# Three more Strassen steps in B's and the FFNs' output products, one column half of the FFNs with its steps in another order, and a new buffer from a smaller dynamic DMA scratch

## The chip, the cores and the metric

The kernel runs on one core of one Trainium2 chip. The metric is the device time of one execution in microseconds, as the median of several runs. Before the change it is 2434.19 us, a median of 3 runs from 2432.38 to 2434.53 us.

## The reference

The program is one layer of a streaming encoder on 256 tokens of width 2048, in float32: a half-weighted SwiGLU feed-forward block (FFN), a mixer with two attention branches A and B, cross attention to 256 memory tokens, and a second FFN, each followed by a layer norm over the scaled residual.

```python
h = layer_norm(ALPHA * h + 0.5 * swiglu_ffn(h, ffn1_w_in, ffn1_w_out), ...)
mix = (g_a * (A(h) @ w_o_a) + g_b * (B(h) @ w_o_b)) @ w_out
h = layer_norm(ALPHA * h + mix, ...)
xa = memory_cross_attention(h, mem, ...)        # ... @ w_xo
h = layer_norm(ALPHA * h + xa, ...)
h = layer_norm(ALPHA * h + 0.5 * swiglu_ffn(h, ffn2_w_in, ffn2_w_out), ...)

def swiglu_ffn(x, w_in, w_out):
    g, u = jnp.split(x @ w_in, 2, axis=-1)      # 5504 columns each
    return (jax.nn.silu(g) * u) @ w_out
```

The three products that matter here are `ffn1_w_out`, `w_o_b` (2048 x 2048) and `ffn2_w_out` (5504 x 2048).

## The kernel before

Every large product runs in split precision. A float32 operand is cut into a high part (a cast to `fp32r`, done by ACT at L262 for weights, L253 for activations) and a low part (what is left, a subtraction by DVE at L265 or L254), and a product is three matmuls: high by high, low activation by high weight, high activation by low weight. The two parts of a weight lie in the tiles `hi` and `lo`, of which there are two each (`UNITS`); a raw weight of 1 MB lies in one of three `raw` tiles, loaded from HBM by SP's queue (L191). A new load starts when the DVE has read the last of the weight that lay in the tile. SP's queue also carries the DMA transposes (L845).

The work goes in **steps**. One step is two blocks of 128 rows of a weight, by 1024 columns, for all 256 tokens. `pair_group` (L643) lays out the steps of one group of 1024 columns, which has 4 output tiles in PSUM (two halves of tokens by two of columns). A plain step is `mm_pair` (L301): 8 block products of three matmuls, so 24 matmuls of 512 columns (L309). A Strassen step is `mm_sums` (L345): its 2 x 2 blocks need 7 block products, 21 matmuls (L363). It takes sums of weight blocks, which the DVE forms (`weight_sums`, L244, at L246 and L248) and splits like a weight into two tiles (for instance X2 and X3), and sums of activation blocks, here called **forms** (`sum_forms`, L314, at L319 and L323, split at L253 and L254), which are kept in a buffer called the form's home. Four of its products go to four shared PSUM tiles `qs`; after a group's last Strassen step `shared` (L669) reads these (L674 to L679) and combines them. The tables `SUMS_OUT`, `AT_YB` and so on say which steps of a group are Strassen steps. Two kinds of PSUM tile, `mm` and `at`, of four each, take turns as a group's own and as its shared tiles.

The instructions of an engine stand in a fixed order when the program is built. The order is made by a scheduler from the order of the calls and from priorities. So an instruction that must wait holds up all that stands behind it on its engine, and a changed step can move its neighbours.

Three places are touched:

- **FFN output, first 24 row blocks** (`ffn`, L551): 12 steps in each of two column halves. Steps 3, 5, 7 and 9 are Strassen steps in both. Behind a half, `finish` (L743) adds the four output tiles to the residual `h` (L749).
- **B's output** (`out_b`, L1268): two column halves of 8 steps, `w_o_b`. Steps 2, 4 and 6 are Strassen steps in the first half, 4 and 6 in the second. Its `done` (L1271) adds the shared tiles (L1276), multiplies by the gate (L1277), adds A's half (L1278), and ACT then splits the words into planes (L841). They are transposed by a DMA, joined again by ACT (L849) and split (L253, L254) into the blocks X0, X1, T0 and X3 of the next product's operand.
- **`w_out`** (`out`, L1316) follows directly: 8 steps for each column half. Its steps 0 to 3 read X0 and X1, made from the first half of B's output; its steps 4 and 5 read T0, and 6 and 7 X3, made from the second. Into its steps are woven the statistics of the memory's layer norm (`mem_norm`, BN_STATS at L387), whose inputs `mem` and `memT` POOL's queue loads (L1334, L1336).

Of the kernel before, what the change touches and what calls it, by code (L numbers as in the profile page):

```python
# [28 lines left out]
AT_FIRST = 4, 6  # L29
SUMS_OUT = ({3: ("X1", 0), 5: ("X1", 1), 7: ("X0", 0), 9: ("X0", 1)},  # L30
            {3: ("X1", 0), 5: ("X1", 1), 7: ("X0", 0)})
SUMS_YB = {4: ("T0", 0), 6: ("T0", 1), 2: None}
AT_YB = (2, 4, 6), (4, 6)
SUMS_XQ = {4: ("H5", 0), 6: ("H5", 1), 2: None}
SUMS_XV = {4: ("T3", 0), 6: ("T3", 1), 2: None}
SUMS_XO = {2: None, 4: ("H2", 0), 6: ("H2", 1)}
# [3 lines left out]
SUM_HOME = ("X2", "X3"),  # L40
# [59 lines left out]
class Kernel:  # L100
# [450 lines left out]
    def ffn(self, tag, xT, st, first=None, steps=None, late=None, before=None, tags=None):  # L551
# [5 lines left out]
        fx = {}  # L557
        for half, nf in enumerate(F_SPLIT):
# [33 lines left out]
            def out(hid=hid):  # L592
                x = lambda: hid
                src = [t[tag + "_w_out"][g, :, f0 * 1024:(f0 + nf) * 1024] for g in range(2)]
                self.out_pair(bank, src[0], 0, nf, x, homes, fh, half == 0, st if end else None,
                              SUM_HOME + ("H5",) if end else SUM_HOME)
                if end:
                    self.out_proj(tag + "_w_out_r", nf, x, False, st, steps, tags, 2, cut=tags is None)
                else:
                    self.out_pair(bank ^ 1, src[1], 1, nf, x, homes, fh, half == 0, None)  # L600
            main = self.collect(out)

            side = dict(turn)
# [2 lines left out]
            for c, (home, k) in homes.items():  # L606
                if home == "X0":
                    side[4 + 2 * k] = side.get(4 + 2 * k, []) + [form(c)]
            if not end:
                for i in range(2):  # L610
                    side[len(main) - 3 + i] = [self.forms_step(fx, SUMS_IN, tuple(SUMS_IN)[i], xT)]
            self.weave(main, side, prio=0)
            turn = None
            f0 += nf

    def out_pair(self, bank, src, g, nk, x, at, fx, scale, st, sums_in=SUM_HOME):

        nc, h = self.nc, self.h
        ps, qs = {}, {}

        def shared():
            for (tt, a), s in qs["add"].items():
                c = (2 * g + a) * 512
                hs = h[tt][:, c:c + 512]
                if scale:
                    nc.vector.scalar_tensor_tensor(hs, hs, ALPHA, s, ALU.mult, ALU.add)
                else:
                    nc.vector.tensor_tensor(hs, hs, s, ALU.add)

        def finish():  # L630
            for tt in range(2):
                for a in range(2):
                    self.finish(tt, 2 * g + a, ps[tt, a], scale and not at, st)
        self.pair_group(bank, src, 512, nk, x, at, fx, ps, qs, shared, sums_in)
        self.add(finish)

    def group_tile(self, j):
# [2 lines left out]
    def group_tiles(self, j):  # L640
        return {(tt, g): self.group_tile(j) for tt in range(2) for g in range(2)}

    def pair_group(self, bank, src, n, nk, x, at, fx, ps, qs, then=None, sums_in=SUM_HOME):  # L643


        steps = -(-nk // 2)
        sums = [c for c in range(steps) if c in at]
        for c in range(steps):
            kts = range(2 * c, min(2 * c + 2, nk))
            ap = src[:, kts[0] * 2 * n:(kts[-1] + 1) * 2 * n]  # L650
            if c in at:
                def fn(w, c=c):
                    if c == sums[0]:
                        qs.update((a, self.group_tile(bank + 1)) for a in range(4))
                    self.mm_sums(ps, qs, w, n, x(), fx[c], 2 * c, c == sums[0], c == sums[-1])
                self.add(fn, Sums(ap, *sums_in))
                if c == sums[-1]:
                    self.add(lambda: self.shared(qs, n), prio=SOON)
                    if then:
                        self.add(then)  # L660
                continue

            def fn(w, c=c, kts=kts):
                if c == 0:
                    ps.update(self.group_tiles(bank))
                self.mm_pair(ps, w, n, x(), kts, c == 0, c == steps - 1)
            self.add(fn, ap)

    def shared(self, qs, n):  # L669
# [1023 lines left out]
def _layout(i):  # L1693
    import numpy as np
    a = {k: np.asarray(v) for k, v in i.items()}
    r = {}
# [5 lines left out]
    for f in ("ffn1", "ffn2"):  # L1702
        w = a[f + "_w_in"][0]
        r[f + "_w_in"] = _pairs(
            w[:, D_FF:D_FF + NG * 512], w[:, :NG * 512], 512, [AT_FIRST] + [SUMS_IN] * (NG - 1))
        r[f + "_w_in_r"] = _pairs(
            w[:, D_FF + NG * 512:], w[:, NG * 512:D_FF], D_FF - NG * 512, [SUMS_IN])
        w = a[f + "_w_out"][0]
        at = [*SUMS_OUT[0], *(F_SPLIT[0] // 2 + c for c in SUMS_OUT[1])]
        r[f + "_w_out"] = _pairs(*_halves(w), 512, [at, at])  # L1710
        r[f + "_w_out_r"] = _tok(w[F_SPLIT[0] * P:, D // 2:])
    r["ffn2_gate"] = _tok(a["ffn2_w_in"][0][:, :512])
    r["ffn2_up"] = _tok(a["ffn2_w_in"][0][:, D_FF:D_FF + 512])
# [57 lines left out]
```

## Time and profile before

| | |
|---|---|
| median of 3 runs | 2434.19 us (2432.38 to 2434.53) |
| the profiled execution: span of its instructions | 2432.9 us; its own time beside the span is not listed |
| PE (matmul) busy | 2423.0 us, 11286 matmuls |
| DVE busy | 2121.1 us |
| ACT busy | 1551.3 us |
| POOL busy | 36.1 us |
| SP's DMA queue (q1) | 495.83 MB |

The span runs from the first to the last instruction of the profiled execution. A row of the timeline has the start in us, the duration, the engine, the source line, the operation with output and input names, the shape and a count of instructions that follow each other; in brackets stands the idle time before it and what ended that. A window row has the busy time of each engine in a stretch. Durations of back-to-back instructions overlap a little: an engine takes up the next one some 0.1 us before the last one's recorded end.

### The profile page before, as it was taken

The page shows a single profiled execution, that of the slowest core. Times are in us where ns is not written, and L with a number is a line of the kernel's source. Part 1 is how long each engine was busy: PE and PEld are TensorE (multiplying, and loading weights), DVE is VectorE, ACT ScalarE, POOL GpSimd, SP SyncE. Part 2 cuts the span into 40 slices and gives each one's busy share as a digit, 9 for nine tenths or more (in the row PEclk, how much of TensorE's full clock was granted, in tenths as well). Part 3 has the DMA queues.
Part 4 walks back from the last instruction along what each step waited for, and adds up shares of the span by engine and source line. Part 5 has one row for each costly group of instructions (what it writes and reads, how often), then busy time and mean ns, then how long its engine had stood idle before and what let it go on. Part 6 is the DMA issues. An engine that isn't in the chain of part 4 may idle for free.

```text
span 2432.9 us, 29701 instructions
## 1 busy us (share of the span) xinstructions
PE 2423.0 (100%) x11286; PEld 2022.5 (83%) x11286; DVE 2121.1 (87%) x2423; ACT 1551.3 (64%) x2017; POOL 36.1 (1%) x81
## 2 busy tenths in 40 slices
PE   9999999999999999999999999999999999999999
PEld 8888888889888888888888888888888888888887
DVE  8999989899878898789788889979879999888997
ACT  6676745666555557878565687765666675556762
POOL 0000000000000001000000000000000000000000
PEclk9999999999999999999999999999999999999999
DMA  7766656666645657776577577655556666666665
GB/s 268 252 214 213 208 199 221 212 199 222 225 172 209 208 209 248 230 209 175 184 249 251 167 236 218 219 184 189 190 199 214 229 221 210 216 208 205 201 223 182
DMA packets 176414, 516.20 MB, mean 212 GB/s; under 512 B 111728, under 2 KB 112496, under 8 KB 121104
## 3 DMA queue, kind: packets, MB, share of 16 engines
q1 hardware_dynamic: 170816, 495.83, 61.2%
q0 software_dynamic: 4592, 17.30, 2.2%
q8 instruction: 88, 1.44, 0.2%
q10 hardware_dynamic: 864, 1.18, 0.1%
q14 instruction: 54, 0.44, 0.1%
HBM read 485.30 MB, written 2.10 MB: 200 GB/s over the span
## 4 chain that ended last, share of the span: by engine, by line
PE 90%; DVE 4%; ACT 3%; DMA 1%; issue 1%; SPq 0%; DVEq 0%; ACTq 0%
PE at L309 24%; PE mm L309 23%; PE mm L296 11%; PE at L363 10%; PE mm L363 10%; PE mm L275 5%; PE mm L277 2%; DVE lo L265 2%; ACT hi L262 1%; PE at L1028 1%; DMA raw<-w_xq 0%; PE at L1499 0%; PE at L1082 0%; PE at L275 0%; DMA raw<-w_o_b 0%
## 5 line engine op out<-in xcount | busy, mean ns | idle before, releaser
L262 ACT CAST hi<-raw 128x1024 fp32r<-128x1024 f32 (+1 forms) x852 | 805.3, 982 | 454.2 <-PE at L309 155.0
L265 DVE TENSOR_TENSOR lo<-raw,hi 128x2048 fp32r<-128x2048 f32 (+1 forms) x427 | 902.3, 2114 | 139.3 <-ACT hi L262 133.4
L309 PE MATMUL mm<-hi,T 128*128 128x512 f32 (+1 forms) x1328 | 311.1, 384 | 1.3 <-DVE v L397 1.3
L309 PEld LDWEIGHTS mm<-hi,T 128*128 128x128 f32 x1328 | 247.3, 188 | 48.5 <-DVE v L397 1.8
L309 PE MATMUL at<-hi,T 128*128 128x512 f32 x1152 | 275.5, 389 | 0.0
L262 ACT CAST X<-H 128x1024 fp32r<-128x1024 f32 (+1 forms) x166 | 170.6, 1034 | 162.0 <-DVE H L246 128.1
L309 PEld LDWEIGHTS at<-hi,T 128*128 128x128 f32 x1152 | 216.2, 188 | 45.1
L265 DVE TENSOR_TENSOR X<-H,X 128x2048 fp32r<-128x2048 f32 (+1 forms) x83 | 186.7, 2250 | 68.6 <-ACT X L262 68.6
L309 PE MATMUL mm<-lo,T 128*128 128x512 f32 (+1 forms) x664 | 160.4, 382 | 0.0
L309 PEld LDWEIGHTS mm<-lo,T 128*128 128x128 f32 x664 | 123.7, 188 | 22.8
L309 PE MATMUL at<-lo,T 128*128 128x512 f32 x576 | 142.4, 389 | 0.0
L309 PE MATMUL at<-hi,H 128*128 128x512 f32 x560 | 133.7, 389 | 0.0
L309 PEld LDWEIGHTS at<-lo,T 128*128 128x128 f32 x576 | 108.1, 188 | 22.5
L309 PEld LDWEIGHTS at<-hi,H 128*128 128x128 f32 x560 | 104.9, 188 | 21.6
L309 PE MATMUL mm<-hi,H 128*128 128x512 f32 x480 | 115.5, 391 | 0.3 <-DVE w L679 0.3
L248 DVE TENSOR_TENSOR H<-H,raw 128x512 f32<-128x512 f32 (+1 forms) x166 | 112.2, 676 | 2.2
L309 PEld LDWEIGHTS mm<-hi,H 128*128 128x128 f32 x480 | 89.5, 188 | 19.3 <-DVE w L679 0.8
L246 DVE TENSOR_TENSOR H<-raw 128x1024 f32<-128x1024 f32 (+1 forms) x83 | 99.4, 1198 | 0.9 <-DMA raw<-w_gate 0.8
L363 PE MATMUL mm<-X,X 128*128 128x512 f32 x342 | 91.1, 392 | 0.0
L262 ACT CAST X<-raw 128x1024 fp32r<-128x1024 f32 (+1 forms) x54 | 55.4, 1036 | 48.7 <-DVE raw L248 38.7
L363 PE MATMUL at<-X,X 128*128 128x512 f32 (+1 forms) x315 | 82.5, 386 | 0.9 <-DVE X L265 0.5
L849 ACT COPY w<-w 128x1024 uint16<-128x1024 uint16 (+1 forms) x60 | 75.8, 1276 | 0.6 <-DMA w<-w 0.5
(373 smaller groups left out, 4123.1 us busy)
## 6 DMA issues: line engine op xcount, KB each, us to landing
raw<-ffn_w_in SPq DMA_DIRECT2D x150, 1024.0 KB, 4.8
raw<-ffn_w_out SPq DMA_DIRECT2D x66, 1024.0 KB, 4.8
raw<-w_gate SPq DMA_DIRECT2D x32, 1024.0 KB, 4.8
raw<-ffn_w_out_r SPq DMA_DIRECT2D x16, 1024.0 KB, 4.9
raw<-w_qk SPq DMA_DIRECT2D x16, 1024.0 KB, 5.5
raw<-w_o_b SPq DMA_DIRECT2D x16, 1024.0 KB, 4.8
raw<-w_out SPq DMA_DIRECT2D x16, 1024.0 KB, 5.2
raw<-w_xk SPq DMA_DIRECT2D x16, 1024.0 KB, 5.3
```

The lines of the kernel that those rows point to most:

```text
L246: self.nc.vector.tensor_tensor(two[0], two[1], raw[:, :m].unsqueeze(1).to_broadcast([P, 2, m]), ALU.add)
L248: self.nc.vector.tensor_tensor(t[:, a * m:a * m + m], t[:, b * m:b * m + m], raw[:, a * m:a * m + m], ALU.add)
L262: self.last_hi = self.nc.scalar.copy(hi[:, c:d], src[:, c:d])
L265: self.last_lo = self.nc.vector.tensor_tensor(lo[:, :n], src, hi[:, :n].bitcast(F32), ALU.subtract)
L275: self.nc.tensor.matmul(ps, hi[j], x.both(kt), start=(j == 0), stop=False)
L277: self.last_mm = self.nc.tensor.matmul(ps[:, :S], lo[j], x.at(0, kt), start=False, stop=(j == n - 1))
L296: self.last_mm = self.nc.tensor.matmul(ps, x.at(xi, kt)[:, tt * P:(tt + 1) * P], w[wi][:, j * 512 + c:j * 512 + c + m], start=(start and j ...
L309: self.last_mm = self.nc.tensor.matmul(ps[tt, g][:, :n], x.at(xi, kt)[:, tt * P:(tt + 1) * P], w[wi][:, c:c + n], start=first and j + wi + ...
L363: self.last_mm = self.nc.tensor.matmul(bank[:, :m], a[xi], v[wi][:, c * m:(c + 1) * m], start=own and first and wi + xi == 0, stop=own and ...
L849: self.nc.scalar.copy(self.words(u, n).rearrange("p (c k) -> p k c", k=2), self.words(s, n).rearrange("p (k c) -> p k c", k=2))
L1028: nc.tensor.matmul(ps[:, c0:c0 + nk], q[:, tt * P:(tt + 1) * P], k[:, :nk], start=(j == 0), stop=(j == len(parts) - 1))
```

## The change

It does four things. The second column half of B's output has a third Strassen step, step 2, whose forms are those that the first half used already. In both FFNs, the second column half of the first 24 row blocks has a fifth Strassen step, step 1, and goes through its steps in the order 0, 3, 2, 5, 4, 7, 6, 9, 8, 1, 10, 11. The forms of step 1 are made while that half runs, in a new buffer F of 8 KB per partition. And the part of each SBUF partition that is kept for the descriptors of POOL's DMAs goes down to 4096 bytes; the library's default is 16384.

```diff
+SUMS_MORE, ORDER_MORE = {1: ("F", 0)}, (0, 3, 2, 5, 4, 7, 6, 9, 8, 1, 10, 11)
 SUMS_YB = {4: ("T0", 0), 6: ("T0", 1), 2: None}
-AT_YB = (2, 4, 6), (4, 6)
+AT_YB = (2, 4, 6), (2, 4, 6)
...
                 else:
-                    self.out_pair(bank ^ 1, src[1], 1, nf, x, homes, fh, half == 0, None)
+                    self.out_pair(bank ^ 1, src[1], 1, nf, x, {**homes, **SUMS_MORE}, fh, True, None, order=ORDER_MORE)
...
             if not end:
+                side[18] = [self.forms_step(fh, SUMS_MORE, 1, lambda hid=hid: hid)]
...
-    def pair_group(self, bank, src, n, nk, x, at, fx, ps, qs, then=None, sums_in=SUM_HOME):
+    def pair_group(self, bank, src, n, nk, x, at, fx, ps, qs, then=None, sums_in=SUM_HOME, order=None):
...
-        steps = -(-nk // 2)
-        sums = [c for c in range(steps) if c in at]
-        for c in range(steps):
+        order = range(-(-nk // 2)) if order is None else order
+        sums = [c for c in order if c in at]
+        for i, c in enumerate(order):
...
-            def fn(w, c=c, kts=kts):
-                if c == 0:
+            def fn(w, i=i, kts=kts):
+                if i == 0:
                     ps.update(self.group_tiles(bank))
-                self.mm_pair(ps, w, n, x(), kts, c == 0, c == steps - 1)
+                self.mm_pair(ps, w, n, x(), kts, i == 0, i == len(order) - 1)
...
-        r[f + "_w_out"] = _pairs(*_halves(w), 512, [at, at])
+        r[f + "_w_out"] = _pairs(*_halves(w), 512, [at, [*at, *SUMS_MORE]])
...
-    nc = bacc.Bacc("TRN2", target_bir_lowering=False, num_devices=1)
+    nc = bacc.Bacc("TRN2", target_bir_lowering=False, num_devices=1, dynamic_dma_scratch_size=4096)
```

`out_pair` passes the order on. Lines of the changed kernel are numbered one or two higher: L246, L248, L265, L309 and L319 become L247, L249, L266, L310 and L320, and L676, L749, L1276 and L1278 become L678, L751, L1278 and L1280.

What the change moves stands in the program's order, engine by engine. PE has 9 matmuls fewer, 3 at each place, and the rest in nearly the same order. The first place is the DVE where the first FFN goes from the first column half of its output to the second. Here `mm_2037` to `mm_2040` are the first half's four output tiles; `lo_2448` is the low part of the second half's step 0. Before:

```order
L265 TENSOR_TENSOR lo_2448<-raw_2445,hi_2447 128x2048
L749 TENSOR_TENSOR h_101<-h_101,mm_2037 128x512
L749 TENSOR_TENSOR h_101<-h_101,mm_2038 128x512
L265 TENSOR_TENSOR lo_2479<-raw_2476,hi_2478 128x2048
L749 TENSOR_TENSOR h_102<-h_102,mm_2039 128x512
L749 TENSOR_TENSOR h_102<-h_102,mm_2040 128x512
L246 TENSOR_TENSOR raw_2524<-raw_2522 128x1024
```

And in the changed kernel, where the next weight is that of step 3:

```order
L266 TENSOR_TENSOR lo_2448<-raw_2445,hi_2447 128x2048
L247 TENSOR_TENSOR raw_2454<-raw_2452 128x1024
L320 TENSOR_TENSOR w_396_2610<-H_104_717 128x512
L249 TENSOR_TENSOR raw_2454<-raw_2454,raw_2452 128x512
L266 TENSOR_TENSOR lo_2483<-raw_2452,hi_2482 128x1536
L249 TENSOR_TENSOR raw_2454<-raw_2454,raw_2452 128x512
L751 TENSOR_TENSOR h_101<-h_101,mm_2037 128x512
L751 TENSOR_TENSOR h_101<-h_101,mm_2038 128x512
L266 TENSOR_TENSOR X_372_2488<-raw_2454,X_371_2487 128x2048
L751 TENSOR_TENSOR h_102<-h_102,mm_2039 128x512
L751 TENSOR_TENSOR h_102<-h_102,mm_2040 128x512
L266 TENSOR_TENSOR lo_2527<-raw_2524,hi_2526 128x2048
```

The Strassen step's weight sums, its two low parts and the start of the new forms stand ahead of the last two additions to `h` now, and these additions are what frees the `mm` tiles for the step's shared products.

The second place is the DVE in B's output, second column half: `lo_9940` and `lo_9989` before, `lo_9956` after, are low parts of plain steps, `H_924` and `H_930` the gates' tile. Before, steps 1, 2 and 3 are plain:

```order
L265 TENSOR_TENSOR lo_9940<-raw_9937,hi_9939 128x2048
L1277 TENSOR_TENSOR H_924_6149<-H_924_6149,w_1564_9906 128x512
L265 TENSOR_TENSOR lo_9989<-raw_9986,hi_9988 128x2048
L1278 TENSOR_TENSOR H_924_6149<-H_924_6149 128x2x512
L265 TENSOR_TENSOR lo_10020<-raw_10017,hi_10019 128x2048
L246 TENSOR_TENSOR X_1579_10026<-raw_10024 128x1024
```

In the changed kernel step 2's weight sums, its low part and the low part of its sums come in:

```order
L266 TENSOR_TENSOR lo_9956<-raw_9953,hi_9955 128x2048
L1279 TENSOR_TENSOR H_930_6165<-H_930_6165,w_1570_9922 128x512
L249 TENSOR_TENSOR X_1575_9962<-X_1575_9962,raw_9960 128x512
L1280 TENSOR_TENSOR H_930_6165<-H_930_6165 128x2x512
L249 TENSOR_TENSOR X_1575_9962<-X_1575_9962,raw_9960 128x512
L266 TENSOR_TENSOR lo_10009<-raw_9960,hi_10008 128x1536
L266 TENSOR_TENSOR X_1583_10014<-X_1575_9962,H_1582_10013 128x2048
L266 TENSOR_TENSOR lo_10045<-raw_10042,hi_10044 128x2048
L247 TENSOR_TENSOR X_1588_10051<-raw_10049 128x1024
```

The low part of step 3 (`lo_10020` before, `lo_10045` after) stands behind them. Its end frees the `raw` tile into which SP loads the weight of step 6. The orders of POOL and of SP's queue stay as they were in these places, so the two transposes that stand behind that load on SP's queue still do.

More of the change, by code (lines that the diff above doesn't have):

```diff
@@ L614, in ffn, with out_pair @@
             f0 += nf
-    def out_pair(self, bank, src, g, nk, x, at, fx, scale, st, sums_in=SUM_HOME):
+    def out_pair(self, bank, src, g, nk, x, at, fx, scale, st, sums_in=SUM_HOME, order=None):
         nc, h = self.nc, self.h
@@ L633, in finish @@
                     self.finish(tt, 2 * g + a, ps[tt, a], scale and not at, st)
-        self.pair_group(bank, src, 512, nk, x, at, fx, ps, qs, shared, sums_in)
+        self.pair_group(bank, src, 512, nk, x, at, fx, ps, qs, shared, sums_in, order)
         self.add(finish)
```

## The prediction

> **What bounds the kernel now.** I read the page's first two parts, then PE's waits, then the chain of waits, then windows at the three places.
>
> ```profile
> span 2432.9 us, 29701 instructions
> PE 2423.0 (100%) x11286; PEld 2022.5 (83%) x11286; DVE 2121.1 (87%) x2423; ACT 1551.3 (64%) x2017; POOL 36.1 (1%) x81
> PEclk9999999999999999999999999999999999999999
> ...
> PE mm L309 <- DVE v L397: 1.3, 1, 1.3
> ...
> 319.25 16.32 PE at L309 x72
> ...
> 319.09:381.65 62.56, 62.56 (x277) 51.80 (x276) 53.19 (x49) 31.61 (x35) 0.00 (x0) 1.00 0.59 202
> 1242.98:1285.14 42.16, 42.16 (x187) 34.91 (x186) 36.87 (x33) 30.51 (x35) 1.59 (x3) 1.00 0.83 276
> 2060.36:2122.92 62.56, 62.56 (x278) 51.80 (x277) 53.28 (x49) 31.62 (x35) 0.00 (x0) 1.00 0.60 205
> ```
>
> PE is busy in all but 9.9 us of the span, at a full granted clock throughout. Its longest wait is 1.3 us. From the chain, a matmul of 512 columns costs 16.32 / 72 = 0.2267 us. The windows are, in the program's order, FFN1's output half, B's second half and FFN2's output half (A, B and C below), each from its first matmul to its last. After the window's length stand the busy times of PE, PEld, DVE, ACT and POOL. PE has no gap in any of them. The DVE has 62.56 - 53.19 = 9.37 us free in A, 5.29 in B and 9.28 in C. So the time falls with every matmul that goes, until a wait takes its place; the DVE is the engine to look at.
>
> **The change part by part.** Three matmuls go at each place, 3 x 0.2267 = 0.68 us, so 9 x 0.2267 = **2.04 us** leave PE. What the DVE gets is priced from its groups:
>
> ```profile
> L265 DVE TENSOR_TENSOR lo<-raw,hi 128x2048 fp32r<-128x2048 f32 x296 | 676.4, 2287 | 125.2 <-ACT hi L262 123.4 <-PE at L363 1.1
> L265 DVE TENSOR_TENSOR lo<-raw,hi 128x1536 fp32r<-128x1536 f32 x123 | 215.4, 1751 | 14.0 <-ACT hi L262 10.0 <-PE mm L309 3.3 <-PE at L309 0.4
> L265 DVE TENSOR_TENSOR X<-H,X 128x2048 fp32r<-128x2048 f32 x77 | 176.2, 2288 | 65.7 <-ACT X L262 65.7
> L248 DVE TENSOR_TENSOR H<-H,raw 128x512 f32<-128x512 f32 x154 | 105.6, 686 | 2.2
> L246 DVE TENSOR_TENSOR H<-raw 128x1024 f32<-128x1024 f32 x77 | 93.7, 1217 | 0.9 <-DMA raw<-w_gate 0.8
> L323 DVE TENSOR_TENSOR w<-w,w 128x128 f32<-128x128 f32 x78 | 22.0, 282 | 0.3
> L319 DVE TENSOR_TENSOR w<-H 128x512 f32<-128x512 f32 x19 | 13.0, 682 | 0.0
> ```
>
> The number behind the busy time is the mean of one in ns. A plain step costs the DVE one subtraction of 2048, 2.29. A Strassen step costs 1.22 (L246) + 2 x 0.69 (L248) + 1.75 (low part of 1536) + 2.29 (low part of the sums). The difference is 1.22 + 1.37 + 1.75 + 2.29 - 2.29 = **4.34 us**. A and C also make the forms: one L319 at 0.68, four L323 at 0.28 and a split, taken like L319 at 0.68, so 2.48 more. ACT's added casts are under 3 us against 31 us free in A and C and 42.16 - 30.51 = 11.65 in B, so they cost nothing unless a cast stands ahead of one that the DVE needs.
>
> *A and C.* 4.34 + 2.48 = 6.82 us fit into 9.37 and 9.28 free. The risk is local. The second Strassen product group starts right after step 0, and its fourth shared tile is an `mm` tile that the last L749 frees.
>
> ```profile
> 314.84 2.28 DVE L265 TENSOR_TENSOR lo<-raw,hi 128x2048 fp32r<-128x2048 f32 x1
> 318.61 1.28 DVE L749 TENSOR_TENSOR h<-h,mm 128x512 f32<-128x512 f32 x2 [1.49 <-PE mm L309]
> ...
> 2057.50 2.29 DVE L265 TENSOR_TENSOR lo<-raw,hi 128x2048 fp32r<-128x2048 f32 x1
> ```
>
> PE needs that tile after step 0 (24 matmuls, 5.44 us) and the 11 matmuls that fill the first three tiles (2.49): at 319.09 + 7.93 = 327.02 in A, at 2060.36 + 7.93 = 2068.29 in C. The DVE, from the low part of step 0 on, has in the new order 2.28 + 1.22 + 0.68 + 0.69 + 1.75 + 0.69 + 1.28 + 2.29 + 1.28 = 12.16 us, and takes each of the 10 that follow up some 0.06 early (below, the row at 1304.01 starts 0.08 before the end of 1301.80 + 2.29), say 11.6. In A it ends at 326.4 to 327.0, in time. In C it starts 2.86 ahead of PE's step 0, not 4.25, and ends at 2069.1 to 2069.7, or 0.8 to 1.4 late. The pick-up is the rough part: at 0.12 each the sum is 11.1, and C's price 0.3. An earlier start of the row isn't to be expected, since nothing ahead of 2057.50 changes. I take **0.7** for C, the middle, and 0 for A, and keep 0 to 1.4.
>
> *B.* Here the end isn't PE's. What follows in `w_out` waits for the DVE:
>
> ```profile
> 1242.50 1.28 DVE L1276 TENSOR_TENSOR w<-w,mm 128x512 f32<-128x512 f32 x2 [0.64 <-PE mm L309]
> ...
> 1254.29 2.29 DVE L265 TENSOR_TENSOR lo<-raw,hi 128x2048 fp32r<-128x2048 f32 x1
> ...
> 1259.57 1.76 DVE L265 TENSOR_TENSOR lo<-raw,hi 128x1536 fp32r<-128x1536 f32 x1 [0.41 <-PE at L309]
> ...
> 1267.21 1.23 DVE L246 TENSOR_TENSOR X<-raw 128x1024 f32<-128x1024 f32 x1 [3.68 <-DMA raw<-w_o_b]
> ...
> 1278.46 2.29 DVE L265 TENSOR_TENSOR lo<-raw,hi 128x2048 fp32r<-128x2048 f32 x1 [0.82 <-ACT hi L262]
> ...
> 1283.57 0.68 DVE L676 TENSOR_TENSOR w<-w,mm 128x512 f32<-128x512 f32 x1
> ...
> 1296.63 1.21 DVE L1278 TENSOR_TENSOR H<-H 128x1024 f32<-128x1024 f32 x1
> 1301.80 2.29 DVE L265 TENSOR_TENSOR lo<-raw,hi 128x2048 fp32r<-128x2048 f32 x1 [3.96 <-ACT hi L262]
> 1304.01 2.46 DVE L387 BATCH_NORM_STATS2 bn<-T 128x6 f32<-128x512 f32 x4
> 1306.39 2.27 DVE L265 TENSOR_TENSOR lo<-raw,hi 128x2048 fp32r<-128x2048 f32 x1
> 1308.75 0.63 DVE L254 TENSOR_TENSOR T<-H,T 128x512 fp32r<-128x512 f32 x1
> ...
> 1306.94 1.15 PE L309 MATMUL mm<-hi,T 128*128 128x512 f32 x4
> 1309.43 1.89 PE L309 MATMUL mm<-hi,T 128*128 128x512 f32 x7 [1.34 <-DVE v L397]
> ```
>
> PE's wait of 1.34 at 1309.43 is named after L397, which ends in the same instant; what PE lacked is the block T0, split at 1308.75 (L254). Behind it the trace goes back without a wait for PE: the low part at 1301.80 waited for ACT, whose cast stands behind L841, which needs the gated sum of 1296.63 (L1278), which needs L676 at 1283.57, all DVE work in a row. So if PE comes 0.68 earlier and the DVE's row isn't earlier, B gains nothing: the wait grows by 0.68. If the row comes later by d, it grows by 0.68 + d in all.
>
> d is the added 4.34 less the idle time that the DVE can use before 1283.57. Between 1242.50 and there it is 0.41 + 3.68 + 0.82 = 4.91, so d lies between 4.34 - 4.91 = **-0.57** and **4.34**. It hangs on the 3.68, a wait for step 6's weight:
>
> ```profile
> 1255.46 1.48 SPq L191 DMA_DIRECT2D raw<-w_o_b  x2
> 1256.99 10.08 SPq L845 DMA_TRANSPOSE H<-H  x2
> ...
> 1254.33 0.53 POOL L1334 DMA_DIRECT2D T<-mem  x1 [98.81 <-DVE H L1278]
> ...
> q0 software_dynamic: 144, 1.05, 51.0%
> ...
> raw<-w_o_b SPq DMA_DIRECT2D x1, 1024.0 KB, 10.5
> ...
> raw<-w_o_b SPq DMA_DIRECT2D x16, 1024.0 KB, 4.8
> ```
>
> Its load, the second of the two SP issues from 1255.46, was sent when the low part of step 3 (1254.29) freed the tile, at 1256.6, and landed 10.5 us later, at 1267.1. In the 5.4 us from there on, POOL's load of `mem` (q0) took 51% of the DMA engines. The usual `w_o_b` load takes 4.8. In the new order step 3's low part stands 4.34 later, so the load starts at about 1260.9. At 4.8 it lands at 1265.7, before the DVE asks at about 1267.3, and the idle 3.68 and 0.41 are worked away: d = 4.34 - 4.09 = 0.25. At 10.5 it lands at 1271.4 and d is 4.34. The `mem` load was issued at 1254.33. If it lands in twice the usual 4.8 at the latest, it is over by 1263.9, so at most half of the new load's way is shared, and it takes 4.8 to 6.4. I take the end near the 4.8 row: **d = 0.25**, with -0.57 to 4.34 for the range. The transposes behind it on SP (1256.99) and the load of step 7 behind these move by the same time; this load was sent at 1267.17, would be at 1271.5, and lands at 1276.3 by the 4.8 row, where its weight's subtraction stands at 1278.46 now. That costs nothing, or a part of the 0.82 that I didn't count as free.
>
> [...] The 51.0% of q0 in this case's window agrees with an even share. [...]
>
> *Smaller scratch.* Nothing in the trace is bound by POOL's queue: 17.30 MB and 4592 packets on q0 in all, 2.2% of the DMA engines' time.
>
> ```profile
> q0 software_dynamic: 4592, 17.30, 2.2%
> ```
>
> The last `mem` load is issued at 1285.61 and read by L387 at 1304.01, so a load that started one landing later would still be in time. I take 0; the upper end is below.
>
> **Sum.** -2.04 + (0.68 + 0.25) at B + 0.7 at C = **-0.4 us**. The profiled execution has a span of 2432.9, 1.3 below the median of 2434.19 and within the runs' 2432.38 to 2434.53; the shift is applied to the median: **2433.8 us**.
>
> **The rivals.**
>
> *R1, slower: B's whole debt goes on the path.* The load of step 6 takes as long as before though it starts later, for the transposes share its queue and POOL's `memT` load follows `mem`. Then T0 comes 4.34 later: -2.04 + 0.68 + 4.34 + 0.7 = +3.7, or 2437.9. It decides from the point where that load lands after about 1267.3. For it: two transposes were in flight in the same 10.5 us. Against it: they stand behind the load on its queue, and twice the usual time is what one rival of equal share explains.
>
> *R2, all of it hidden.* The DVE also works through the 0.82 it waited for ACT before 1283.57, and in C the tile comes free in time: -2.04 + 0.68 - 0.57 = -1.9, or 2432.3. For it: 4.91 us of idle time stand against 4.34 of work. Against it: the 0.82 waits for ACT's cast, which has new work ahead of it, and C's row sum ends late by either pick-up time. B's own 0.68 stays lost here too, since T0's row goes on from DVE to DVE.
>
> *R3, the smaller scratch makes POOL wait for descriptors.* It would hold back a `mem` load until an earlier one has landed, and L387 stands ahead of T0's split on the DVE. From 1285.61 to 1304.01 are 18.4 us, which is room for one held landing, not for three. Where it fell through, one more landing of 5 to 10 us would go on the path: about 2442. The trace shows no POOL wait of this kind, so it has a small chance.
>
> [...]
>
> That the change doesn't do what it says is excluded by the order of PE, which has 9 matmuls fewer.
>
> **How the numbers follow.** Forecast 0.52 (B between 0 and 1.5, C anywhere in its bound), R2 0.25, R1 0.20, R3 0.03. To hold 8 in 10, the range takes in R2's 2432.3 less 0.7 for the spread of the runs, 2431.6, and reaches to R1 less half of C's price, 2437.6, which leaves out R3 and R1's upper part. About 0.2% (4.9 us) is what a measurement of this kernel can tell from no change: below 2429.3 counts as faster, above 2439.1 as slower. The forecast, R1 and R2 all lie inside. Faster gets 0.03, since even -2.04 doesn't reach it; slower gets R3 and a rest of R1, 0.05; same 0.92.
>
> **What would show it.** PE has 9 matmuls less. The wait before L309 with T in `w_out` is longer, 1.34 + 0.68 + d; d is read from the start of B's shared additions (L676, 1283.57 now), and its cause from the idle time ahead of step 6's first sum and the landing of its load. If PE waits at the fourth shared tile at the start of A or C, the price there is read from that gap. If PE waits elsewhere, for a low part or an X in A or C, the free 9 us were not where I took them to be, and the prediction is wrong. If POOL's issues of `mem` come later than 1285.6 by several us, R3 holds.

## The result, and the profile after

The changed kernel takes **2440.25 us** (median of 11 runs, 2433.71 to 2445.75), the kernel before beside it 2433.9 us (11 runs, 2432.38 to 2435.93). The ratio is 1.0023, with a 95% interval from 1.0013 to 1.0032: slower, by about what the measurement can tell. In two later runs of the same kernel it came out at 1.0009 [1.0001, 1.0018] and 1.0015 [1.0005, 1.0025], with medians of 2435.51 and 2435.43. The forecast was 2433.8, in a range that ended at 2437.6.

The median hides the main thing: the executions of the changed kernel differ by 12 us, those of before by 3.6. An execution of over 2438 us is called long here, the others short. Of the 33 executions in these three runs 13 are long (7, 2 and 4 of 11), so the median depends on how many of them a run happens to have. The profile of this run fell on a short one (2433.79 us). Its page:

```profile
span 2432.0 us, 29717 instructions
PE 2421.7 (100%) x11277; PEld 2020.1 (83%) x11277; DVE 2135.3 (88%) x2447; ACT 1555.6 (64%) x2025; POOL 36.0 (1%) x81
PEclk9999999999999999999999999999999999999999
```

PE has 9 matmuls fewer (11286 to 11277), the DVE 24 instructions more, and the span is 0.9 us shorter, not longer. So the work that the change adds doesn't lengthen every execution; the loss is in some of them. A profile of a long one came with a later run of the same kernel (`e14_after_mark`, span 2439.2). PE's waits there, with the engine and instruction that ended them:

```profile
PE mm L364 <- ACT H L263: 4.4, 2, 4.2
PE at L491 <- DVE w L468: 1.1, 1, 1.1
PE mm L310 <- ACT T L254: 1.0, 1, 1.0
```

In the short execution the first of these isn't among the waits, and the longest is the 1.1 which the kernel before has too, at its L490. The 4.2 us are one wait, in B's second half, at the product of step 6's weight sums. What happened there, short and long, on SP's queue, ACT and PE. In the short execution:

```profile
1259.40 4.83 SPq L847 DMA_TRANSPOSE H<-H  x2
1264.35 0.51 SPq L192 DMA_DIRECT2D raw<-w_o_b  x1
...
1270.69 1.06 ACT L263 CAST H<-X 128x1024 fp32r<-128x1024 f32 x1 [1.35 <-DVE X L247]
1272.80 2.00 ACT L263 CAST hi<-raw 128x1024 fp32r<-128x1024 f32 x2 [1.05 <-DMA raw<-w_o_b]
1274.70 1.04 ACT L263 CAST H<-X 128x1024 fp32r<-128x1024 f32 x1
...
1279.38 0.96 PE L364 MATMUL mm<-X,T 128*128 128x512 f32 x3 [0.76 <-DVE X L266]
```

And in the long one, where also the DVE's rows are shown:

```profile
1259.37 7.31 SPq L847 DMA_TRANSPOSE H<-H  x2
1266.80 0.51 SPq L192 DMA_DIRECT2D raw<-w_o_b  x1
...
1271.42 1.05 ACT L263 CAST H<-X 128x1024 fp32r<-128x1024 f32 x1 [0.57 <-DVE X L247]
1277.69 1.99 ACT L263 CAST hi<-raw 128x1024 fp32r<-128x1024 f32 x2 [5.23 <-DMA raw<-w_o_b]
1279.59 1.04 ACT L263 CAST H<-X 128x1024 fp32r<-128x1024 f32 x1
...
1279.72 2.29 DVE L266 TENSOR_TENSOR lo<-raw,hi 128x2048 fp32r<-128x2048 f32 x1 [5.98 <-ACT hi L263]
1281.92 2.28 DVE L266 TENSOR_TENSOR X<-X,H 128x2048 fp32r<-128x2048 f32 x1
...
1280.68 1.22 PE L364 MATMUL mm<-H,T 128*128 128x512 f32 x2 [4.15 <-ACT H L263]
```

The reader is to follow one row down. The two transposes of words of B's first half hold SP for 7.31 us instead of 4.83, so the load behind them, of step 7's weight, is issued at 1266.80 instead of 1264.35. It then takes 10.9 us to the start of its casts (1277.69) where it took 8.4 (1272.80). Between the two `H<-X` rows, the casts of the two halves of step 6's weight sums, ACT's fixed order has the casts of step 7's weight. So the second half, ready at 1273.7 (the DVE's last L249), is cast at 1279.59 instead of 1274.70, and PE, which reads it, stands for 4.15 us. The low part of these sums (the row at 1281.92) stands behind the low part of step 7 on the DVE in the same way.

The wait isn't the whole price. The granted clock in stretches of 3.4 us around it, in the long execution (columns as in the prediction; the last three are the granted clock, the DMA engines' share and GB/s):

```profile
1272.80:1276.20 3.40, 3.40 (x17) 2.76 (x15) 0.94 (x2) 0.00 (x0) 0.53 (x1) 1.00 0.99 376
1276.20:1279.60 3.40, 0.33 (x2) 0.00 (x0) 0.00 (x0) 1.91 (x3) 0.00 (x0) 1.00 1.01 422
1279.60:1283.00 3.40, 2.32 (x6) 1.83 (x7) 3.28 (x2) 3.40 (x6) 0.00 (x0) 0.51 0.98 407
1283.00:1286.40 3.40, 3.40 (x10) 2.63 (x9) 2.51 (x3) 2.69 (x4) 0.00 (x0) 0.50 0.92 325
1286.40:1289.80 3.40, 3.40 (x16) 2.84 (x15) 2.83 (x3) 2.00 (x3) 0.00 (x0) 0.99 0.01 5
```

After a stretch in which PE worked 0.33 of 3.40 us, the granted clock is 0.51 and 0.50 in the next two, and 10 matmuls take the time of 16. PE works for 2.32 + 3.40 = 5.72 us of these two, and half of that, 2.9 us, is what the clock costs. Wait and clock come to 4.2 + 2.9 = 7.1 us; the short execution waits 0.76 in the same step, at its row 1279.38, so that 6.3 of the 7.2 us are found here by which this span (2439.2) stands over the short one (2432.0). Where the rest goes wasn't followed.

The clock goes with the time in the executions without a profile too: all 13 long ones of the 33 have a mean granted clock of 0.997 to 0.999, and 19 of the 20 short ones have 1.000. No profile fell on an execution over 2442.4 us, so what the longest ones do (up to 2446.99) isn't shown.

### The profile page after: what moved, and what is told of

Read it like the earlier page. It is cut to its first block, busy times and chain, and to the rows that moved or that the text cites. A ratio compares the mean times of both kernels' runs of the same rounds, so it can differ in the third digit from the quotient of the medians.

```text
span 2432.0 us, 29717 instructions
## 1 busy us (share of the span) xinstructions
PE 2421.7 (100%) x11277; PEld 2020.1 (83%) x11277; DVE 2135.3 (88%) x2447; ACT 1555.6 (64%) x2025; POOL 36.0 (1%) x81
## 4 chain that ended last, share of the span: by engine, by line
PE 89%; ACT 4%; DVE 3%; DMA 2%; issue 1%; SPq 0%; DVEq 0%; ACTq 0%
PE at L310 24%; PE mm L310 23%; PE at L364 11%; PE mm L364 11%; PE mm L297 11%; PE mm L276 5%; PE mm L278 2%; ACT hi L263 2%; DVE lo L266 1%; PE at L1030 1%; DMA raw<-w_xq 1%; ACT H L851 1%; PE at L1501 0%; PE at L1084 0%; PE at L276 0%
## 5 line engine op out<-in xcount | busy, mean ns | idle before, releaser
L266 DVE TENSOR_TENSOR lo<-raw,hi 128x2048 fp32r<-128x2048 f32 (+1 forms) x427 | 901.0, 2111 | 130.0 <-ACT hi L263 125.6
L310 PE MATMUL mm<-hi,T 128*128 128x512 f32 (+1 forms) x1328 | 311.3, 383 | 1.7 <-DVE v L398 0.8
L310 PEld LDWEIGHTS mm<-hi,T 128*128 128x128 f32 x1328 | 247.0, 188 | 49.5 <-DVE v L398 1.2
L310 PE MATMUL at<-hi,T 128*128 128x512 f32 x1136 | 272.1, 389 | 0.0
L310 PEld LDWEIGHTS at<-hi,T 128*128 128x128 f32 x1136 | 213.2, 188 | 44.6
L266 DVE TENSOR_TENSOR X<-H,X 128x2048 fp32r<-128x2048 f32 (+1 forms) x83 | 186.8, 2251 | 70.2 <-ACT X L263 70.2
L310 PE MATMUL mm<-lo,T 128*128 128x512 f32 (+1 forms) x664 | 160.4, 382 | 0.0
L310 PEld LDWEIGHTS mm<-lo,T 128*128 128x128 f32 x664 | 123.7, 188 | 22.8
L310 PE MATMUL at<-lo,T 128*128 128x512 f32 x568 | 140.4, 389 | 0.0
L310 PE MATMUL at<-hi,H 128*128 128x512 f32 x528 | 126.3, 389 | 0.0
L310 PEld LDWEIGHTS at<-lo,T 128*128 128x128 f32 x568 | 106.6, 188 | 22.1
L310 PE MATMUL mm<-hi,H 128*128 128x512 f32 x480 | 115.5, 391 | 0.4 <-DVE w L681 0.4
L310 PEld LDWEIGHTS at<-hi,H 128*128 128x128 f32 x528 | 98.9, 188 | 20.3
L249 DVE TENSOR_TENSOR H<-H,raw 128x512 f32<-128x512 f32 (+1 forms) x166 | 112.5, 678 | 2.3
L310 PEld LDWEIGHTS mm<-hi,H 128*128 128x128 f32 x480 | 89.6, 188 | 19.3 <-DVE w L681 0.8
L247 DVE TENSOR_TENSOR H<-raw 128x1024 f32<-128x1024 f32 (+1 forms) x83 | 99.5, 1199 | 1.0 <-DMA raw<-w_gate 0.9
```

The source lines that it names most:

```text
L247: self.nc.vector.tensor_tensor(two[0], two[1], raw[:, :m].unsqueeze(1).to_broadcast([P, 2, m]), ALU.add)
L249: self.nc.vector.tensor_tensor(t[:, a * m:a * m + m], t[:, b * m:b * m + m], raw[:, a * m:a * m + m], ALU.add)
L266: self.last_lo = self.nc.vector.tensor_tensor(lo[:, :n], src, hi[:, :n].bitcast(F32), ALU.subtract)
L310: self.last_mm = self.nc.tensor.matmul(ps[tt, g][:, :n], x.at(xi, kt)[:, tt * P:(tt + 1) * P], w[wi][:, c:c + n], start=first and j + wi + ...
```

## The experiments

Fifteen runs, in four groups, in the order of the table: four, four, four and three. The runs of a group shared one chip and the runs of the kernel before. The last column counts the long executions (over 2438 us); of the 112 of the kernel before beside them it is one (2438.47).

| run | median (lowest to highest), n | before beside it | ratio, 95% interval | over 2438 |
|---|---|---|---|---|
| `e0_again` | 2435.51 (2433.97 to 2438.65), 11 | 2433.46 | 1.0009 [1.0001, 1.0018] | 2 |
| `e1_scratch` | 2433.29 (2432.72 to 2435.09), 11 | 2433.46 | 1.0000 [0.9991, 1.0008] | 0 |
| `e2_b` | 2442.93 (2435.49 to 2446.60), 6 | 2433.46 | 1.0036 [1.0024, 1.0048] | 4 |
| `e3_ffn` | 2431.94 (2431.03 to 2435.49), 11 | 2433.46 | 0.9996 [0.9988, 1.0005] | 0 |
| `e4_send` | 2436.09 (2433.44 to 2442.13), 11 | 2433.98 | 1.0010 [1.0001, 1.0019] | 2 |
| `e6_order` | 2439.43 (2437.85 to 2447.79), 6 | 2433.98 | 1.0032 [1.0020, 1.0044] | 5 |
| `e5_24` | 2435.22 (2433.16 to 2437.55), 11 | 2433.98 | 1.0003 [0.9995, 1.0012] | 0 |
| `e7_late` | 2442.15 (2437.01 to 2451.93), 7 | 2433.98 | 1.0043 [1.0026, 1.0059] | 5 |
| `e2_again` | 2436.36 (2435.07 to 2442.40), 11 | 2433.78 | 1.0014 [1.0005, 1.0023] | 3 |
| `e8_memT` | 2436.92 (2434.59 to 2438.77), 11 | 2433.78 | 1.0014 [1.0006, 1.0023] | 3 |
| `e9_both` | 2435.52 (2433.72 to 2436.74), 11 | 2433.78 | 1.0007 [0.9998, 1.0016] | 0 |
| `e10_24` | 2432.91 (2431.45 to 2433.53), 11 | 2433.78 | 0.9996 [0.9988, 1.0005] | 0 |
| `e12_b_order` | 2436.05 (2433.48 to 2446.91), 11 | 2433.62 | 1.0015 [1.0005, 1.0024] | 4 |
| `e13_after_order` | 2435.93 (2433.19 to 2444.37), 10 | 2433.62 | 1.0013 [1.0003, 1.0023] | 3 |
| `e14_after_mark` | 2435.43 (2433.42 to 2446.99), 11 | 2433.62 | 1.0015 [1.0005, 1.0025] | 4 |

### Which part of the change

`e0_again` is the changed kernel. The others of this group are the kernel before with `dynamic_dma_scratch_size=4096` (`e1_scratch`), the kernel before with

```diff
-AT_YB = (2, 4, 6), (4, 6)
+AT_YB = (2, 4, 6), (2, 4, 6)
```

(`e2_b`), and the changed kernel with this line undone (`e3_ffn`).

> The changed kernel once more, for the profile of a long execution. Its eleven executions ran from 2433.7 to 2445.8 with granted clocks from 1.000 to 0.998, the longer the lower, while those of before stayed within 2432.4 to 2435.9. Theory S (smaller scratch): a POOL transfer is late in the long executions. Theory B: PE waits for T0 in w_out longer than 1 us in them, because step 6's weight or the transposes land late. Theory F: PE waits in one of the FFN halves. In each, PE stands some us and its clock is lowered behind the wait. All three expect the spread again, a median of 2436 to 2443; a profile above 2436 would show the place.

> The kernel before with the smaller scratch alone. Theory S: the spread of the changed kernel, a median of 2437 to 2444 (2 us above that, since no matmul goes). Theories B and F: as before, 2433 to 2435, within 3.5 us of each other.

> The kernel before with B's third Strassen step alone, scratch of 16384 bytes. Theory B: the spread and a median of 2436 to 2444. Theories S and F: 2433 to 2435.5 with a narrow spread (my forecast's term for B was 0.25 over before).

> The changed kernel without B's third Strassen step: both FFN steps, their order and the smaller scratch. Theory F or S: spread, a median of 2436 to 2444. Theory B: narrow, 2432.5 to 2434 (-1.36 from PE, up to 0.7 given back at C).

`e0_again` came out below the 2436 that all three theories had, and its profile fell on a short execution, so it didn't show the place. For the smaller scratch no difference is measured. The FFN steps take 1.5 us off the median, to 2431.94, a little under what theory B had (the interval of the ratio still holds 1). B's third step alone brings the spread and the loss, so S and F fall. Of theory B the place stands; that T0 is what PE waits for isn't shown by this, and the long execution above shows another product. The profile of `e2_b` fell on a short execution too. Its longest wait, 1.4 us at L275, lies at 1399 us, far behind B; the new wait inside B's output pointed to a place:

```profile
PE mm L363 <- DVE X L265: 0.8, 1, 0.8
```

### What of B's step

In that trace the low part of step 6's sums, called X3, stands on the DVE behind the low part of step 7, whose weight is loaded behind the transposes. Three edits of `e2_b` (or of before) and one that makes it worse. `held_ap` marks step 7's weight; the line that sets it, the line of `AT_YB` where it is as in `e2_b`, and the smaller scratch of `e7_late` are left out:

```diff
# e4_send: the transposes behind step 7's load
-            return {2: [send(0)], 4: [send(1)], 5: [turn(0)], 6: [turn(1)]}
+            return {2: [send(0)], 5: [turn(0)], 7: [send(1)], 8: [turn(1)]}
...
# e6_order: in load(), step 7's casts and low part behind X3
+                if ap is getattr(self, "held_ap", None):
+                    first = self.last_lo
...
# e5_24: of before
-AT_YB = (2, 4, 6), (4, 6)
+AT_YB = (2, 4, 6), (2, 4)
...
# e7_late: in fetch(), a load of 1 MB ahead of step 7's
+                if ap is getattr(self, "held_ap", None):
+                    with self.tc.issue_after(self.sent.ins):
+                        self.sent = self.nc.sync.dma_start(self.block("F", (P, 2048)), ap)
```

> B's third step alone, but the second pair of DMA transposes is issued behind the load of step 7's weight instead of ahead of it. In the trace of B's step alone, the DVE's low part of step 6's sums (X3) stands behind the low part of step 7, which waits for that load, and PE waits 0.8 us for X3. Theory W (in long executions step 7's weight lands later, X3 is late, PE stands and its clock is lowered): the load starts some 5 us earlier, no wait for X3, narrow, 2433 to 2435. Theory T (T0 in w_out is late in long executions, through the DVE's debt): still spread, a median of 2438 to 2444.

> B's third step alone, but step 7's two casts and its low part are ordered behind the low part of step 6's sums on ACT and the DVE, as in the kernel before. Theory W: X3 no longer waits for step 7's weight, narrow, 2433 to 2435. Theory T: spread, a median of 2438 to 2444, since step 7's weight and T0 come as late as before.

> Two Strassen steps in B's second half as in the kernel before, but steps 2 and 4 in place of 4 and 6. PE has as many matmuls as before. There is no sum of step 6 behind step 7's weight. Theory W: narrow, 2433 to 2435. Theory that an early Strassen step (step 2) with its debt on the DVE is the cause: spread, over 2437.

> B's third step alone (with the scratch of 4096 bytes for room), and an extra load of 1 MB, which nothing reads, on SP ahead of step 7's weight, so that this lands some 2.5 to 5 us later. Theory W: PE's wait for X3 grows from 0.8 to 3 to 6 us in every execution and the granted clock falls behind it; 2440 to 2447 with the profile showing both. Theory T: the wait for T0 takes the same 3 us at most: 2436 to 2439, clock 1.000.

`e5_24` is free of long executions, with a median 0.2 above what theory W gave: an early Strassen step with its debt on the DVE isn't enough for the loss. A Strassen step just ahead of step 7 isn't either, since the kernel before has one; only the kernels with all three show it.

`e4_send` missed: its median is above the 2435 that theory W gave and under theory T's 2438, and two executions are over 2438. In its profile, of a short execution, PE doesn't wait for X3. Its ratio, 1.0010, is below `e2_b`'s 1.0036, but B's step alone came out at 1.0014 in the next group (`e2_again`), so that even an improvement isn't shown. `e7_late` is as slow as `e2_b` and reaches higher, 2451.93; its profiled execution, at span 2435.6, was a short one and showed waits of 1.2 and 1.1 us only, not the 3 to 6 that I expected in every execution. Step 7's casts start 2.4 us later there than in `e2_b` (1275.96 against 1273.52), about the least that the edit was to bring, and the two waits are together 1.5 us longer than `e2_b`'s 0.8.

`e6_order` went against me: 5 of 6 executions are long. Its profile, of the shortest of them, shows one reason. The edit also pushed the low part of `w_out`'s step 0 behind additions of B's output, and PE waits for that:

```profile
PE mm L311 <- DVE lo L267: 3.4, 1, 3.4
```

So it tells nothing of the order that it was made for. It does show the clock's part once more, in stretches from the wait on:

```profile
1288.90:1292.30 3.40, 0.18 (x1) 0.00 (x0) 3.40 (x4) 1.99 (x2) 0.00 (x0) 1.00 0.66 205
1292.30:1295.70 3.40, 3.21 (x8) 2.53 (x9) 3.40 (x4) 1.99 (x2) 0.00 (x0) 0.51 0.97 219
1295.70:1299.10 3.40, 3.40 (x16) 2.81 (x15) 2.88 (x2) 1.99 (x2) 0.00 (x0) 0.99 1.00 398
```

### A long execution, and repairs of the transfers

`e2_again` is `e2_b`; it came out as expected, at 2436.36 with a spread of 7.3 us. `e8_memT` is `e2_b` with

```diff
-                nc.gpsimd.dma_start(e["m"][j], t["mem"][j])
+                d = nc.gpsimd.dma_start(e["m"][j], t["mem"][j])
+                e["last"] = e.get("last", d)
             for j in range(2):
-                nc.gpsimd.dma_start(e["raw"][j], t["memT"][:, 8 * j:8 * j + 8, :])
+                with self.tc.issue_after(e["last"].ins):
+                    nc.gpsimd.dma_start(e["raw"][j], t["memT"][:, 8 * j:8 * j + 8, :])
```

`e9_both` is the changed kernel with this and the edit of `e4_send`; `e10_24` is the changed kernel with `AT_YB = (2, 4, 6), (2, 4)`.

> B's third step alone once more, as the mark for the runs beside it on the same chip: 2436 to 2444, spread over 6 us or more.

> B's third step alone, with POOL's two loads of memT behind its second load of mem (so after about 1285 instead of at 1263 and 1273). They then share the DMA engines no longer with the load of step 7's weight (1265 to 1273) and the transposes. Theory C (the sharing with memT makes step 7's weight late in long executions): narrow, 2433 to 2435.5. Otherwise (the queue of transposes ahead of that load is enough): spread as before, a median of 2438 to 2444.

> The changed kernel with both repairs: the second pair of transposes behind step 7's load, and memT behind mem. If lateness of step 7's weight is the whole cause: 2431.5 to 2433.5, narrow, about 2 us under the kernel before where the matmuls' 2.04 us come through at A and C and B gives nothing: -1.4. If T0's wait has a spread of its own: 2433 to 2437 with some executions near 2440.

> The changed kernel with B's second half back to two Strassen steps, at 2 and 4 instead of 4 and 6: both FFN steps stay. From the FFN steps alone (-1.5 against before) and from steps 2 and 4 alone (+1.2): 2432.5 to 2434. If an early Strassen step in B is harmless by itself: 2431.5 to 2432.5.

This time the profile of B's step alone fell on a long execution (span 2440.6). It has the chain of the long execution above, with larger numbers: SP's transposes, the casts of step 7's weight, and PE:

```profile
1260.25 8.85 SPq L845 DMA_TRANSPOSE H<-H  x2
1269.22 0.51 SPq L191 DMA_DIRECT2D raw<-w_o_b  x1
...
1279.64 1.99 ACT L262 CAST hi<-raw 128x1024 fp32r<-128x1024 f32 x2 [5.22 <-DMA raw<-w_o_b]
...
1282.63 1.22 PE L363 MATMUL mm<-H,T 128*128 128x512 f32 x2 [4.56 <-ACT H L262]
```

`e8_memT` is not narrow: its highest execution is lower (2438.77 against 2442.40), its median isn't, and three are long in each. Theory C alone doesn't hold. But its profile, of a short execution, bears on the question of what makes the weight late:

```profile
1268.53 0.51 SPq L191 DMA_DIRECT2D raw<-w_o_b  x1
...
1274.12 1.99 ACT L262 CAST hi<-raw 128x1024 fp32r<-128x1024 f32 x2
```

Step 7's load was sent later here than in the long execution of the changed kernel (1266.80), and its casts start 5.6 us later, not 10.9; PE doesn't wait for X3. So a late issue behind the transposes wasn't enough by itself: the load's own time, with `memT` beside it, is part of the lateness.

With both repairs (`e9_both`) no execution is over 2438; but the median stays 1.7 us over before, where theory W has 0.3 to 2.3 us under it. It lies where a spread of T0's own was to put it, without the executions near 2440 that this was to bring. In its profile, a short execution (span 2433.2), the longest wait is T0's again: in B and `w_out` PE waits for 0.79, 0.31 and 1.34 us, in the kernel before for 1.34 alone. Four of its executions, from 2435.58 to 2436.74, have a granted clock of 0.999, so the lowered clock isn't gone. The changed kernel itself wasn't run in this group, and it had only 2 long ones of 11 in `e0_again`; none of 11 is no proof of a repair. `e10_24` came out narrow, within the first of its two forecasts: the whole gain that is left is that of the FFNs.

### The order alone

Step 7's casts behind the last cast of step 6's sums, and its low part behind X3, in `e2_b` (`e12_b_order`) and in the changed kernel (`e13_after_order`):

```diff
+                kept, x3 = self.chain, ap is getattr(self, "held_ap", None)
+                if x3:
+                    first, self.chain = self.last_hi, self.last_lo
                 with self.tc.issue_after(first.ins) if first else nullcontext():
                     got = self.halves(raw[:, :ap.shape[1]], hi, lo)
+                self.chain = kept
```

> B's third step alone, with step 7's low part ordered behind the low part of step 6's sums (X3) on the DVE and its casts behind those of X3 on ACT; the low part of w_out's step 0 keeps a place ahead of the additions, which the earlier order repair lost. Theory W (long executions come from X3 and its cast standing behind step 7's weight, which waits for the transposes): no execution above 2437.5, clock 1.000, a median of 2433.5 to 2435. If another consumer of the late transposes takes over (X1's split, which stands ahead of w_out's step 0): long executions remain, with PE waiting for that low part.

> The changed kernel with the same order repair. Theory W: 1.4 us under B's step alone with the repair: 2432 to 2434, no execution above 2436. Else spread as in the changed kernel, to 2440 and more.

> The changed kernel once more, as the mark beside the repaired one on the same chip: a median of 2435 to 2441, some executions above 2438.

The order is not the whole cause: the long executions stay, four and three where theory W had none. The profile of `e13_after_order` fell on one (span 2438.8), that of `e12_b_order` on a short one. In the long one X3 is early now, at 1275.22, and PE stands for 3.4 us a little later, for the high part of step 7's weight itself, not for the low part of `w_out`'s step 0 that the other forecast named:

```profile
1275.22 2.29 DVE L270 TENSOR_TENSOR X<-X,H 128x2048 fp32r<-128x2048 f32 x1 [1.12 <-ACT H L267]
...
1282.17 5.54 PE L314 MATMUL at<-hi,T 128*128 128x512 f32 x16 [3.40 <-ACT hi L267]
...
1281.07 1.99 ACT L267 CAST hi<-raw 128x1024 fp32r<-128x1024 f32 x2 [5.88 <-DMA raw<-w_o_b]
```

So of theory W the late weight stands, and X3's place behind it only decides which product of PE waits first.

What makes the weight late is seen in the transfers. From 1264 to 1270, with DMA share and GB/s at the end, the first row is the short execution of the changed kernel, then come the long ones of `e14_after_mark`, `e2_again` and `e13_after_order`:

```profile
1264.00:1270.00 6.00, 6.00 (x27) 4.79 (x27) 6.00 (x4) 5.30 (x7) 0.00 (x0) 1.00 1.09 355
```

```profile
1264.00:1270.00 6.00, 5.80 (x25) 4.35 (x24) 5.82 (x3) 5.06 (x6) 0.00 (x0) 1.00 1.01 66
```

```profile
1264.00:1270.00 6.00, 5.19 (x23) 3.85 (x22) 4.49 (x2) 4.62 (x6) 0.53 (x1) 1.00 1.29 75
```

```profile
1264.00:1270.00 6.00, 5.58 (x25) 4.16 (x24) 5.53 (x3) 4.77 (x6) 0.00 (x0) 1.00 0.95 61
```

The DMA engines are busy in all four (shares of 0.95 to 1.29), but in the long executions they move a fifth of the bytes, 61 to 75 GB/s against 355. In this stretch the two transposes run: they take 5.9 and 8.7 us from issue to landing in the short execution of the changed kernel, 10.8 and 14.0 in the long one, and 11.2 and 12.9 in the profile of before, where PE doesn't wait for what stands behind them. Step 7's load behind them on SP is sent at 1266.80 in the long execution of the changed kernel, at 1264.35 in the short one. Why they are slow in some executions isn't settled: in `e8_memT`, without POOL's load beside them, the stretch shows 172 GB/s, and SP was held 7.43 us.

## Why the prediction was wrong

- **PE's gain** held: 9 matmuls fewer.
- **A and C** came out at 0 in the short execution, where I took 0 and 0.7. In A the last addition that frees the fourth tile ends at 325.39 + 1.28 = 326.67 and PE needs it at 319.37 + 7.93 = 327.30. In C the last one ends at 2067.68, against 2059.84 + 7.93 = 2067.77: I had taken A's order for C, which has no L320 there and the last addition alone behind X's low part. That is 0.6 of the 0.9 us between the 0.8 late that I took at the least and the 0.09 early that it was; the other 0.3 is that the row started 3.19 us ahead of PE's step 0, not 2.86. `e3_ffn` gives -1.5 us for both; PE's gain there is 1.36.

```profile
325.39 1.28 DVE L751 TENSOR_TENSOR h<-h,mm 128x512 f32<-128x512 f32 x2
...
2067.00 0.68 DVE L751 TENSOR_TENSOR h<-h,mm 128x512 f32<-128x512 f32 x1
```

- **B, step 6's load and T0** held in the short execution as far as the DVE goes. It took step 6's weight without a wait (the load's way was 5.2 us, sent at 1259.03), d was swallowed, and T0 is split at 1308.54, 0.2 us earlier than before. (L676, now L678, by whose start I wanted to read d, comes 2.3 us earlier, at 1281.27, because a low part of 2.29 us that stood ahead of it stands behind it now.) PE's waits for T0 are 0.45 and 0.78, not the 1.34 + 0.68 + 0.25 = 2.27 that I forecast: T0 comes 0.46 earlier than I took it to, and PE later, since it waits 0.76 for X3 first.
- **The step that failed** is the sentence on step 7's load: that it "would be at 1271.5, and lands at 1276.3 by the 4.8 row", and that this "costs nothing, or a part of the 0.82". The cost is what was wrong. The landing was less so: the issue came earlier than I took it (1264.35 to 1269.2) and the way was longer than 4.8 (8.4 us in the short execution, 10.8 in the long one; this very load took 7.5 in the trace of before, which I didn't use), so that it landed at 1272.8 and at 1277.6. In the kernel before, step 7's casts start at 1276.43 and nothing waits, because both halves of step 6's sums are cast ahead of them, and PE needs step 7 only at 1279.70:

```profile
1270.46 1.05 ACT L262 CAST H<-X 128x1024 fp32r<-128x1024 f32 x1
1272.00 1.06 ACT L262 CAST H<-X 128x1024 fp32r<-128x1024 f32 x1 [0.49 <-DVE X L248]
...
1276.43 2.00 ACT L262 CAST hi<-raw 128x1024 fp32r<-128x1024 f32 x2
...
1279.70 3.79 PE L309 MATMUL at<-hi,T 128*128 128x512 f32 x16
```

In the changed kernel ACT and the DVE take step 7's weight ahead of the second half of step 6's sums, and PE takes up step 7's high part among the products of step 6, at 1276.86 in the short execution. So PE needs step 7's weight, by way of these sums, about 3 us earlier than before: it stood from 1276.53 in the long execution. There PE went on 3.1 us after the landing (1280.68 against 1277.6). By an estimate from these rows, even the landing that I forecast, 1276.3, would have let PE go on at 1279.4 only, a wait of 2.9 us where I took nothing. The order of B's second half behind step 6 was the part of the change that I hadn't looked at; the measured price is, in the long execution, the wait of 4.2 us and 2.9 us of lowered clock.

- **R1** had the right kind, a load in B that lands late and a slower kernel, but the wrong load (step 6's), the wrong reader (T0 through the DVE) and the wrong price: its 2437.9 has no lowered clock in it. R3 fell with `e1_scratch`; R2's 2432.3 was not reached by any execution of the changed kernel. Two short executions take what the forecast has (2433.71 and 2433.79 against 2433.8); that is no hit, since the forecast was for the median.
- **The range** was built from one profiled execution's durations as if every execution had them. It would have held the medians of the two later runs (2435.51 and 2435.43), which had 2 and 4 long executions instead of 7; that would have been luck, since the step that failed is the same in them. The transposes in the trace of before, 10.08 us on SP, were a sign that they can be slow; I moved them by a fixed time.

What stays open: why the transposes take 5 us on SP in some executions and 7 to 9 in others, how much of step 7's lateness is theirs and how much is `memT`'s, and what `e9_both` still loses. No repair that was tried brings B's third step below the kernel before.

The lowest median is that of the change without B's third step (`e3_ffn`, 2431.94 us against 2433.46 for before and 2435.51 for the changed kernel on the same chip). Its gain over before is within the interval of no difference; that over the changed kernel is 3.6 us in the medians.

## What to carry to other kernels

Where a PE-bound kernel loses matmuls, ask which weight or sum PE reads first behind the shortened step, in the new order of every engine, and how late its load can be before PE stands: here a load behind transposes took 7.5, 8.4 and 10.8 us in three executions. Compare spreads, not medians alone; a change that takes away cover of some 3 us may show it only in some executions. And count the clock: behind PE waits of 3.4 to 4.2 us it was 0.50 to 0.51 here, which by an estimate from PE's busy time cost 1.6 to 2.9 us more.

## What the hardware showed that was not expected

Read in stretches of 3.4 us, the granted clock behind the wait was low for one of them (0.51 in `e6_order`, 0.50 in `e13_after_order`) or for two (0.51 and 0.50 in `e14_after_mark`). In `e13_after_order` the wait of 3.4 us lay across two stretches and filled neither:

```profile
1276.80:1280.20 3.40, 1.89 (x8) 0.90 (x6) 0.71 (x1) 0.00 (x0) 0.00 (x0) 1.00 1.01 422
1280.20:1283.60 3.40, 1.43 (x6) 1.22 (x7) 0.51 (x1) 2.53 (x4) 0.00 (x0) 1.00 1.01 419
1283.60:1287.00 3.40, 3.40 (x9) 2.65 (x9) 3.40 (x4) 3.40 (x5) 0.00 (x0) 0.50 0.86 296
1287.00:1290.40 3.40, 3.40 (x16) 2.73 (x15) 3.11 (x5) 3.40 (x6) 0.53 (x1) 0.99 0.65 270
```

PE was busy for 1.89 us of the first stretch, and the clock was 1.00 in the second; it was busy for 1.43 us of the second, and the clock was 0.50 in the third. In the kernel before, the wait of 1.34 us for T0 left PE busy for 2.06 us of 3.40, with a clock of 1.00 in that stretch and in the 10 us from 1310:

```profile
1307.10:1310.50 3.40, 2.06 (x10) 1.22 (x9) 3.40 (x9) 2.69 (x4) 0.00 (x0) 1.00 0.80 308
1310.00:1320.00 10.00, 10.00 (x45) 8.26 (x44) 7.46 (x14) 7.41 (x9) 0.00 (x0) 1.00 0.70 240
```

The lowered clock did not last equally long. In `e6_order` and `e13_after_order` PE was busy for 3.21 and 3.40 us of the first slow stretch, and the next was at 0.99. In `e14_after_mark` it was busy for 2.32 us of it, and the next was at 0.50 again. Half of PE's busy time in the slow stretches, an estimate of the price from these rows, is 1.6 and 1.7 us in the first two and 2.9 in the third.

From 1264 to 1270, at DMA shares of 0.95 to 1.29, the engines moved 61 to 75 GB/s in three long executions, where short executions of the changed kernel, at 1.09, moved 355 and 335 (`e0_again`). SP was held by the transposes until 1264.23 and 1265.37 in the short ones, until 1266.68, 1269.10 and 1267.55 in the long ones (`e14_after_mark`, `e2_again`, `e13_after_order`).
